# Three sets of projection buffers, a shorter weight path and a contention-aware order in a hybrid decoder layer

## The chip, the cores and the metric

The kernel runs on all 8 cores of one Trainium2 chip, one batch row on each core, with no exchange between cores. The time is device microseconds (us) of the slowest core of one execution. Cores 0 to 3 are one die, 4 to 7 the other. Some executions are of a slower state: part of the cores get a lower granted TensorE clock and are some per cent longer. Such executions are "slow".

Engines: PE is the matmul engine, PEld its weight load, DVE is VectorE, ACT is ScalarE, POOL is GpSimd, SP only issues transfers.

## The reference, cut to what matters

```python
# BATCH 8, SEQ 2048, D_MODEL 1024, 8 query / 2 key heads of 64, LRU_WIDTH 512, D_FF 2816
h = rmsnorm(x, norm_mix_pre)
q, k, v, lx, lg = split(h @ w_in)                     # 1792 columns
attn = sliding_window_attention(q, k, v, sinks)       # window 128, ALiBi, banded blocks of 128
lx = causal_dwconv(lx, lru_conv_w, lru_conv_b)        # 4 taps
lru = rg_lru(lx, wa, ba, wx, bx, lam) * gelu(lg)      # gates, exp, sqrt(1 - a^2), scan along SEQ
merged = concat(rmsnorm(attn, g_attn), rmsnorm(lru, g_lru))
x = x + rmsnorm(merged @ w_out, norm_mix_post)
f = rmsnorm(x, norm_ffn_pre) @ w_up                   # 5632 columns
gate, val = split(causal_dwconv(f, ffn_conv_w, b))    # 3 taps
x = x + rmsnorm((gelu(gate) * val) @ w_down, norm_ffn_post)
```

## The kernel before

The mixer (all up to the first residual) goes through four chunks of 512 positions. Each chunk has five stages: A (norm and transpose of x), B (projection with w_in), D (convolution, gates, scan), C (attention), E (output matmul, two norms, transposes for the FFN). The program builds a graph of operations with a priority (`key`) and, for each, the engines that could do it with a duration; a list scheduler in the same file places them and turns the graph into five in-order instruction streams. A dependency is a tile name, so one buffer under one name also orders the chunks that use it.

The w_in weights go through three f32 staging buffers and are multiplied by the norm gain on the way:

```python
    def stage(src, nbytes, key):
        i = ns[0] % 3
        ns[0] += 1
        dma("sp", stg[i][:], src, nbytes, [], ["stg%d" % i], key, ("stg", i))
        return stg[i], "stg%d" % i
    ...
    for n, fc in enumerate(order):
        s_, sk = stage(win_d[fc].rearrange("p c n -> p (c n)"), 524288, -50 + n)
        f = tt_fn(win[:, fc], s_[:].rearrange("p (c n) -> p c n", c=8), g0b, ALU.mult)
        P.op({"dve": (1.25, f), "pool": (2.4, f)}, [sk, "pp"], [("win", fc)], -50 + n)
```

There is one buffer of each projection result, and the chunks are written out one after the other:

```python
    hT = alloc("hT", [128, 8, 512], BF16)
    qT = alloc("qT", [128, 4, 512], BF16)
    glT = alloc("glT", [128, 4, 512], BF16)
    ...
    wout_load()
    for k in range(NCH):
        stage_a(k)
        stage_b(k)
        stage_d(k)
        stage_c(k)
        ...                                  # for k == 0: xe0, xe1, ye, h2b are placed
        stage_e(k)
```

The convolution reads its input from SBUF, and the output stage goes through one `ye` and one `h2b`:

```python
                for tap in (2, 1, 0):
                    sh = 3 - tap
                    stt(xc[:, cc, :], lx[:, c, o0 - sh:o0 - sh + 512], cw(c, tap), xc[:, cc, :], ALU.mult, ALU.add,
                        512, LXK + ["pp", (nm["xc"], cc)], [(nm["xc"], cc)], key)
    ...
            X, Y, H = xe[t % 2], ye, h2b     # stage_e
```

The softmax here doesn't subtract the row's maximum and nothing guards it: scores larger than these inputs give would overflow.

## Time and profile before

| | before |
|---|---|
| median of 17 executions, us, slow ones included (5 were there at first: 844.23) | 843.12 (839.92 to 919.5) |
| span of the profiled execution, slowest core, us | 840.2 |
| median span of the dies, us | 835.9 and 834.9 |
| PE / DVE / ACT / POOL busy, us | 708 / 487 / 391 / 335 |
| starts of the four output stages, us | 122.3, 205.9, 288.7, 393.0 |
| end of the last transpose for the FFN, us | 446.2 |
| up matmuls done before that end | 336 of 1408 |

The prediction below shows the lines for the main readings (busy tenths, windows, chain, waits). Two groups of the page matter besides. The columns are line, engine, operation, output and inputs, shapes, count, then busy us and mean ns of one, then the idle time just before them with what ended it:

```profile
L442 DVE SCALAR_TENSOR_TENSOR xc<-lx,pp,xc 128x512 f32<-128x512 bf16 x48 | 44.2, 939 | 2.4 <-POOL xc L432 1.2
L422 ACT ACT_TABLE_LOAD x27 | 34.6, 1283 | 20.3 <-DVE T L442 7.5
```

The first is the convolution taps, both tensor inputs in SBUF (the core's on-chip memory), 939 ns in the mean. The second is the activation table loads, 27 of them, with 20.3 us of idle time just ahead.

The last three rows of the table are my way to read a pipeline of stages. They come from the timeline of PE: the first matmul with `wob` of each chunk starts an output stage, and the last transpose with `h2b` ends the mixer. An "up matmul" is one of the 1408 with w_up, the first part of the FFN. After that, PE only has the rest of the FFN.

### The profile page before, as it was taken

The numbers are of one execution on the slowest core, as the hardware profiler recorded it, in microseconds if no ns is written. First come the engines' busy times: TensorE is split into PE (matmuls) and PEld (weight loads), VectorE is DVE, ScalarE is ACT, GpSimd is POOL, SyncE is SP. The second block draws the span as 40 slices with busy tenths as digits, with TensorE's granted clock in tenths as the row PEclk, the third lists the DMA queues.
The fourth block names the chain that finished last, engine by engine and source line by source line (L and its number), as shares of the span: only waits on it lengthen the run. The fifth ranks groups of instructions, "written<-read, shape, count | busy, mean of one in ns | idle before, by whom it ended". The sixth has DMA issues, their size and how long they took to land.

```text
span 840.2 us, 10795 instructions; the slowest of 8 cores (830.9 to 840.2 us)
## 1 busy us (share of the span) xinstructions
PE 708.3 (84%) x3700; PEld 330.7 (39%) x3700; DVE 487.0 (58%) x488; ACT 390.5 (46%) x534; POOL 334.7 (40%) x391
## 2 busy tenths in 40 slices
PE   0394878588848878589888999999999999999995
PEld 0141443334333433234333444444444444444442
DVE  2395854485448556856657777322377777772322
ACT  2247825882587359486344555111144444541111
POOL 4292372536253444736454444301044444442000
PEclk9997899698988999799989999999999999999998
DMA  9877112401320046787863444232254444411231
GB/s 216 257 230 217 52 51 106 144 1 51 114 86 1 2 125 176 106 133 103 186 174 66 79 79 78 53 122 103 101 126 76 75 76 76 76 26 50 101 113 62
DMA packets 25253, 85.52 MB, mean 102 GB/s; under 512 B 3056, under 2 KB 3440, under 8 KB 25072
## 3 DMA queue, kind: packets, MB, share of 16 engines
q0 software_dynamic: 10080, 29.66, 21.6%
q1 hardware_dynamic: 15120, 55.18, 20.0%
q8 instruction: 30, 0.49, 0.3%
q14 instruction: 23, 0.19, 0.1%
HBM read 97.70 MB, written 16.78 MB: 136 GB/s over the span
## 4 chain that ended last, share of the span: by engine, by line
PE 60%; DVE 9%; POOL 8%; issue 8%; ACT 7%; DMA 7%; SPq 0%; POOLq 0%; DVEq 0%; ACTq 0%
PE ps L461 59%; DMA stg<-w_in_r 4%; POOL stats L435 2%; DMA stg<-w_out_r 2%; DVE ye L442 2%; POOL stats L432 2%; POOL xe L435 1%; PE ps L466 1%; ACT xc L422 1%; DVE xc L706 1%; DVE xe L435 1%; ACT PT L422 1%; ACT h2b L422 1%; DVE T L442 1%; ACT L422 1%
## 5 line engine op out<-in xcount | busy, mean ns | idle before, releaser
L461 PE MATMUL ps<-h2T,wu 128*128 128x512 bf16 x1408 | 314.8, 385 | 17.8 <-DVE T L442 11.5
L442 DVE SCALAR_TENSOR_TENSOR T<-ps,pp,T 128x1023 f32<-128x1023 f32 (+1 forms) x176 | 223.9, 1280 | 68.9 <-ACT T L422 33.6
L461 PEld LDWEIGHTS ps<-h2T,wu 128*128 128x128 bf16 x1408 | 138.0, 99 | 188.8 <-issue 31.1
L422 ACT ACTIVATE T<-ps,pp 128x1024 f32<-128x1024 f32 x88 | 105.8, 1203 | 132.0 <-PE ps L461 130.0
L461 PE MATMUL ps<-wdn,uT 128*128 128x512 bf16 x704 | 152.3, 379 | 0.5 <-issue 0.5
L435 POOL TENSOR_TENSOR uT<-gg,T 128x1024 bf16<-128x1024 f32 x44 | 103.7, 2357 | 54.5 <-DVE T L442 49.0
L432 POOL TENSOR_SCALAR stats<-stats 128x1 f32<-128x1 f32 (+1 forms) x72 | 27.5, 381 | 209.5 <-ACT yf L422 128.4
L461 PE MATMUL ps<-hT,win 128*128 128x512 bf16 x416 | 100.5, 399 | 3.7 <-ACT hT L422 1.4
L461 PEld LDWEIGHTS ps<-wdn,uT 128*128 128x128 bf16 x704 | 68.8, 98 | 83.7 <-issue 0.9
L442 DVE SCALAR_TENSOR_TENSOR yf<-ps,stats,g 128x1024 f32<-128x1024 f32 x16 | 20.5, 1284 | 110.7 <-POOL stats L435 110.7
L422 ACT ACTIVATE yf<-ps 128x1024 f32<-128x1024 f32 x16 | 16.4, 1023 | 132.7 <-PE ps L461 132.7
L461 PEld LDWEIGHTS ps<-hT,win 128*128 128x128 bf16 x416 | 40.8, 101 | 54.9 <-issue 14.7
L422 ACT ACTIVATE gg<-T 128x1024 f32<-128x1024 f32 x44 | 46.3, 1053 | 12.7 <-DVE T L442 9.6
L435 POOL TENSOR_TENSOR stats<-stats,nhalf 128x1 f32<-128x1 f32 (+1 forms) x68 | 47.8, 703 | 9.1
L442 DVE SCALAR_TENSOR_TENSOR xc<-lx,pp,xc 128x512 f32<-128x512 bf16 x48 | 44.2, 939 | 2.4 <-POOL xc L432 1.2
L422 ACT ACT_TABLE_LOAD x27 | 34.6, 1283 | 20.3 <-DVE T L442 7.5
L466 PE MATMUL ps<-ident,hb 128*128 128x128 bf16 x128 | 14.8, 293 | 33.8 <-POOL hb L432 33.8
L442 DVE SCALAR_TENSOR_TENSOR h2b<-xe,stats,g 128x1024 bf16<-128x1024 f32 x16 | 22.6, 1411 | 35.2 <-POOL stats L435 35.2
L470 POOL DMA_DIRECT2D wu<-w_up_r x44 | 26.3, 597 | 40.9 <-PE ps L461 39.6
L442 DVE SCALAR_TENSOR_TENSOR ye<-ps,stats,g 128x1024 f32<-128x1024 f32 x16 | 20.5, 1284 | 30.6 <-POOL stats L435 30.6
L466 PE MATMUL ps<-ident,h2b 128*128 128x128 bf16 x128 | 12.0, 249 | 28.1 <-DVE h2b L442 12.1
L435 POOL TENSOR_TENSOR T<-T,carry 128x2 f32<-128x2 f32 x44 | 8.8, 200 | 66.4 <-DVE T L442 66.0
(103 smaller groups left out, 719.2 us busy)
## 6 DMA issues: line engine op xcount, KB each, us to landing
wu<-w_up_r POOLq DMA_DIRECT2D x44, 512.0 KB, 5.2
xt<-x SPq DMA_DIRECT2D x16, 512.0 KB, 5.0
xe<-x SPq DMA_DIRECT2D x16, 512.0 KB, 3.5
out<-xe SPq DMA_DIRECT2D x16, 512.0 KB, 2.7
xf<-out SPq DMA_DIRECT2D x16, 512.0 KB, 3.8
out<-xf SPq DMA_DIRECT2D x16, 512.0 KB, 2.7
stg<-w_in_r SPq DMA_DIRECT2D x14, 512.0 KB, 8.7
wdn<-w_down_r POOLq DMA_DIRECT2D x22, 256.0 KB, 8.9
```

Source lines behind the costliest of these rows:

```text
L422: return e.activation(**kw)
L432: return lambda e: e.tensor_scalar(out=_v(out), in0=_v(in0), scalar1=s1, scalar2=s2, op0=op0, op1=op1)
L435: return lambda e: e.tensor_tensor(out=_v(out), in0=_v(in0), in1=_v(in1), op=op)
L442: return P.op({"dve": (dur, lambda e: e.scalar_tensor_tensor(out=_v(out), in0=_v(in0), scalar=scalar, in1=_v(in1), op0=op0, op1=op1))}, re ...
L461: fns.append(lambda e, o=o, l=l, r=r, s0=s0, s1=s1: e.matmul(_v(o), lhsT=l, rhs=r, start=s0, stop=s1))
L466: fns = [lambda e, o=o, i=i: e.transpose(_v(o), i, ident[:]) for (o, i) in items]
L470: return P.op({eng: (0.6 if eng == "pool" else 0.08, lambda e: e.dma_start(out=out, in_=in_))}, reads, writes, key, dma=nbytes, slot=slot)
L706: P.op({"dve": (1.3, lambda e, cc=cc, init=init, a2=a2, tha=tha, thx=thx: e.tensor_tensor_scan(out=a2[:, cc, :], data0=tha[:, cc, :], data ...
```

## The change

Its intent is to fill PE in the mixer. It does these things together:

- w_in is cast by its transfers straight into place, the tables and later weights wait for pieces of it, and the gains move to the evictions of the transposes;
- three sets of `qT`, `xcb`, `glT` and two `hT`, with the projections of chunks 1, 2 and 3 written ahead of earlier chunks' later stages;
- the convolution runs on the projection's PSUM result, with a small carry for the three columns at a chunk's start;
- the square root becomes exp(0.5 ln), which leaves two activation table sets, and each load is issued ahead of the waits of its activation;
- the scheduler has better durations, a rule that keeps long DVE and POOL operations apart ("the lock rule"), and a penalty for the slower of two engines; two groups of transfers are moved in the order by hand.

The diff, cut to its core (`...` marks cuts; renamed keys, durations and the FFN's buffer places are left out):

```diff
+        def locked(o, e):
+            return e in lockt and len(o.alts[e]) > 2 and o.alts[e][2]
+        fastest = [min(a[0] for a in o.alts.values()) for o in ops]
 ...
+                    if locked(o, e):
+                        st = max(st, lockt["pool" if e == "dve" else "dve"])
 ...
-                if best is None or (pick[0], pick[1].key) < (best[0], best[2].key):
-                    best = (pick[0], e, pick[1])
+                pen = 0.7 * (pick[1].alts[e][0] - fastest[pick[1].idx])
+                if best is None or (pick[0] + pen, pick[1].key) < (best[3], best[2].key):
+                    best = (pick[0], e, pick[1], pick[0] + pen)
 ...
+                        if e == "act" and o.tload:
+                            eng.preload_act_table_set(TABSETS[o.tload])
 ...
+    for i in range(3):
+        INTO.append(cur[0])
+        qTs.append(alloc("qT%d" % i, [128, 4, 512], BF16))
+        xcbs.append(alloc("xcb%d" % i, [128, 4, 512], BF16))
+        glTs.append(alloc("glT%d" % i, [128, 4, 512], BF16))
+    hTs = [alloc("hT%d" % i, [128, 8, 512], BF16) for i in range(2)]
 ...
-    for n, fc in enumerate(order):
-        s_, sk = stage(win_d[fc].rearrange("p c n -> p (c n)"), 524288, -50 + n)
-        f = tt_fn(win[:, fc], s_[:].rearrange("p (c n) -> p c n", c=8), g0b, ALU.mult)
-        P.op({"dve": (1.25, f), "pool": (2.4, f)}, [sk, "pp"], [("win", fc)], -50 + n)
+    for n, fc in enumerate(order):
+        P.tag["win", n] = dma("pool", win[:, fc, :, :], win_d[fc], 524288, [], [("win", fc)], -50 + n, ("win", fc))
 ...
+                for tap in (2, 1):
+                    sh = 3 - tap
+                    stt(T[:, sh:512], pb(g, lambda a, sh=sh: a[:, 0:512 - sh]), cw(c, tap), T[:, sh:512],
+                        ALU.mult, ALU.add, 512, [g, tk, "pp"], [tk], key)
 ...
-            act(a2[:], a2[:], AF.Sqrt, 1024, XC, XC, key + 2, scale=-1.0, bias=1.0, tab=("sqrt",))
+            act(a2[:], a2[:], AF.Ln, 1024, A2, A2, key + 2, scale=-1.0, bias=1.0, tab=("L",))
+            act(a2[:], a2[:], AF.Exp, 1024, A2, A2, key + 2, scale=0.5, tab=("L",))
 ...
-    wout_load()
-    for k in range(NCH):
+    for k in range(3):
         stage_a(k)
         stage_b(k)
-        stage_d(k)
-        stage_c(k)
 ...
+    stage_d(0)
+    stage_c(0)
+    stage_a(3)
+    stage_b(3)
+    stage_e(0)
 ...
```

## The prediction

> **What bounds the kernel now.** I read the clock of the eight cores first (0.942 to 0.952 on both dies: an undisturbed run), then the page, then the windows. On the page, the busy tenths of the slowest core:
>
> ```profile
> PE   0394878588848878589888999999999999999995
> DVE  2395854485448556856657777322377777772322
> ACT  2247825882587359486344555111144444541111
> PEclk9997899698988999799989999999999999999998
> ```
>
> (One digit is 21 us.) PE is full in the right half, at full clock. In the left half no engine is full for long, and the granted clock dips with the holes. The windows view, cut where the character changes, gives the budget:
>
> ```profile
> 0.00:94.00 94.00, 45.55 (x277) 22.11 (x278) 51.66 (x72) 42.69 (x65) 41.62 (x46) 0.91 0.78 217
> 94.00:446.00 352.00, 277.82 (x1653) 134.65 (x1649) 217.95 (x246) 211.20 (x312) 170.69 (x199) 0.90 0.40 95
> 446.00:831.70 385.70, 384.90 (x1778) 173.89 (x1776) 214.88 (x170) 135.51 (x156) 121.65 (x144) 1.00 0.36 81
> 831.70:840.20 8.50, 0.00 (x0) 0.00 (x0) 2.51 (x2) 1.11 (x2) 0.74 (x2) 0.65 0.15 62
> ```
>
> Columns: stretch, length, then busy us of PE, weight load, DVE, ACT, POOL, then clock, DMA share, GB/s. Start (94 us): the DMA is busy 78%. Mixer (352 us): PE 79%, DVE 62%, ACT 60%, clock 0.90; nobody is the bound, they wait for each other. FFN (386 us): PE 99.8%; only fewer matmuls would shorten it. Tail 8.5 us.
>
> The chain that ended last says what the start waits for: weights staged in f32 through three buffers, scaled on DVE or POOL, and the next staging load held back by that scaling.
>
> ```profile
> 3.76 16.02 DMA stg<-w_in_r
> ...
> 21.89 10.95 DMA stg<-w_in_r
> ...
> 59.55 5.43 DMA stg<-w_out_r
> ...
> 73.12 6.52 DMA stg<-w_out_r
> ```
>
> In the mixer stretch the waits view is a ring of short handoffs, and table loads (22 of 27 are there) stand on the chain:
>
> ```profile
> POOL stats L432 <- ACT h2b L422: 40.1, 12, 4.5
> DVE h2b L442 <- POOL stats L435: 35.2, 13, 6.2
> DVE ye L442 <- POOL stats L435: 30.6, 16, 5.6
> ```
>
> Projection buffers (hT, qT, glT) are single, so the next chunk's projection, which would fill PE, cannot run while this chunk's recurrence, attention and output stage pass around that ring. In the chain, the output stage of chunks 0 to 3 starts at 122, 206, 289 and 393 us: a period of 83 us and more.
>
> **What the Trainium skill says.** "ScalarE: Activation LUTs", section "What ACT_TABLE_LOAD costs": about 1283 ns, whatever the set. The trace agrees: 27 loads at a mean of 1283 ns. Its section "Table sets" has exp and ln together in one set, which is what lets the change write the square root as exp(0.5 ln). "TensorE: Matmul & The Clock Gate", section "Back-to-back issue gap": N/2.4 + 2.5 ns, 216 ns at N = 512, in isolation, and less in a sustained stream (131 ns). The trace sides with the first: 187 recorded in a full 40 us window is 214 ns each. "VectorE: DVE Perf Modes", section "Two Vector instructions with no wait between them", has the second SBUF read interface shared with GpSimd, used by ops with two SBUF tensors. The trace fits that: the convolution taps with both tensors in SBUF took 939 ns for 512 columns, while the FFN taps with one tensor in PSUM took 1280 ns for 1023, so some 0.75 us for 512. "DMA: Bandwidth & Descriptors", section "SWDGE vs HWDGE vs iDMA": a cast in flight needs GpSimd's queue. The wu loads already do it, 5.2 us to landing.
>
> **The change, part by part.**
>
> (1) Start. w_in is cast by the DMA straight into its place; the gain moves to the eviction of the transpose. Off go 9 x 1.56 + 5 x 2.06 = 24 us of DVE and POOL work and the three-buffer ring. The bytes stay: 14 x 0.5 MB plus four x tiles of 0.5 MB, 9.4 MB. At the 217 to 257 GB/s of the first slices that is about 40 us, so w_in is complete at about 44 us instead of 58, and the first projection ends near 48. Then comes a catch: on the SP queue the x tiles 6 and 7 stand behind three w_out loads and gbc, and those wait for the last w_in piece. These 3.7 MB take 15 us more; with norm and transposes the second projection starts at about 66 us, where the kernel before got to it at 94. Gain 28 us.
>
> (2) PE work for the rest. Matmul counts do not change. At 0.2157 us: projection 416 = 90, gates 32 = 7, scores 124 = 27, output 256 = 55; V, PV, transposes about 43. Mixer sum 222 us at full clock; FFN 2112 x 0.2157 = 456. The order on PE has 208 up matmuls (45 us) ahead of the last transpose of the last output stage, where before it was some 330 (71 us, from 456 less the 385 of the FFN stretch). So the mixer stretch has 222 + 45 less the 33 done before 66 us = 234 us of full-clock PE work, against some 257 before (check: 277.8 busy x clock 0.90 = 250).
>
> (3) DVE in the mixer, order counts times durations of the rows before. Convolution: 63 us (48 x 0.94, 9 + 9 helpers, 8 lx evictions) becomes 48 x 0.75 = 36. Gain-carrying evictions: 15 become 32 x 1.23 = 39. h2b 22.6 becomes 11 x 0.8 = 9; hb 0 becomes 7; the attention normalisation, now in halves, costs 8 more; w_in off 14. The sum is about 224 against 222: no relief in total. After 66 us some 201 are left, plus 33 for FFN taps: 234, as much as PE.
>
> (4) ACT. 27 loads become 20: minus 9. Convolution start plus 12.6, ln and exp for sqrt plus 8.4, norm scalings plus 7; lx and transposed evictions minus 19. No net change, some 211 us. But each load is now issued ahead of the waits of its activation, so a part of them is hidden. POOL loses some 35 us.
>
> (5) Where the gain really comes from: three sets of qT, xcb, glT and two of hT. On PE's order, projections of chunks 2 and 3 now lie between the score, gate and output matmuls of the chunk before. The stretch becomes limited by throughput (234 us for PE at full clock, 234 for DVE) rather than by the ring. It still has E stages with one ye and one h2b buffer, and for chunks 1 and 2 four output groups back to back on PE which leave at the pace of that one buffer, so PE will not be full. I take 90% PE busy (79% before) and clock 0.92 (0.90): 234 / 0.83 = 282 us.
>
> (6) FFN: 1904 matmuls remain after the last transpose: 411 us. gelu now writes in place, which holds a T buffer until POOL's 2.36 us product is done. A buffer is held some 10 us and two steps take 2 x 16 x 2 x 0.2157 = 13.8, so this hides. Tail 8.5.
>
> Sum: 66 + 282 + 411 + 8.5 = 767. I put 765.
>
> **The rivals.**
> (a) The ring persists: E stages and the recurrence set the period whatever PE has to fill in, or DVE's in-order queue, with conv, gains and FFN taps mixed, holds short links of the chain behind long ones. For it: DVE's sum did not fall, and the gain evictions are now on DVE alone (before, 10 of 32 went to ACT). Then density stays at 0.79 x 0.90: 234 / 0.71 = 329, and the time is 815.
> (b) The order is nearly perfect: better-measured durations (a four-column power is now booked at 1.4 us; the trace has 1.28 and 1.5, the old order assumed 0.35), DVE and POOL kept off each other. 95% busy at clock 0.95 gives 259, and 744.
> (c) The start does not get shorter: transfers of all cores share the memory, and POOL's queue now issues both w_in and the statistics. Then 20 us are lost: 785. Against it: the start is one stretch where bytes alone need 40 us and the kernel took 58.
> (d) The clock: denser matmuls could meet a lower granted clock on all cores. The FFN stretch at 99.8% busy had 1.00, which speaks against it.
>
> **Range and chances.** (a) in part and (c) in part make the upper end, 800; (b) the lower, 735. For no gain of 2% (827) the mixer would have to become looser than before while also starting later; chances 0.96 faster, 0.03 same, 0.01 slower.
>
> **What would show it.** Right: PE continuously busy from about 66 us; the last transpose of h2b at about 345 to 350 us, with DVE near 83% and PE near 90% between; convolution taps near 0.75 us; 20 table loads; the last 420 us as full as before. Wrong: second projection after 80 us (step 1); output stages of successive chunks still 80 us apart or PE under 80% in the mixer (step 5); holes in the FFN stretch (step 6); granted clock under 0.95 there (d).

## The result, and the profile after

The changed kernel is correct and takes 770.66 us (median of 9 executions, 769.84 to 775.89; one more, of 779.24, is not among the nine). A ratio here is the mean time of one kernel's fast runs over that of the other's in the same rounds, so it is not quite the ratio of the medians quoted. It is 0.917 (95% interval 0.915 to 0.919). The profiled execution has a span of 768.8 us, all cores between 761.8 and 768.8 us at a clock of 0.963 to 0.974: an undisturbed run, like that of before.

The busy tenths of the changed kernel's slowest core (one digit is now 19 us):

```profile
PE   1887987898899699989999999999999999999995
...
DVE  3536677854686769687777762223777777752222
ACT  3267889765788766555555441111545455431111
...
PEclk9996999899799879999999999999999999999998
```

PE is at 7 to 9 tenths from the second slice on, with one dip to 6. The windows view, cut at the second projection and at the last transpose, has the same columns as in the prediction:

```profile
0.00:66.60 66.60, 39.56 (x228) 19.98 (x228) 31.26 (x60) 33.98 (x55) 22.98 (x51) 0.93 0.96 222
66.60:347.70 281.10, 252.82 (x1569) 117.88 (x1570) 199.78 (x291) 203.58 (x305) 131.08 (x196) 0.93 0.45 111
347.70:759.40 411.70, 411.15 (x1905) 186.05 (x1902) 234.77 (x184) 150.19 (x176) 133.32 (x153) 1.00 0.38 85
759.40:768.80 9.40, 0.00 (x0) 0.00 (x0) 2.51 (x2) 1.11 (x2) 0.74 (x2) 0.73 0.14 57
```

From 66.6 us to the last transpose PE is busy 252.8 / 281.1 = 90% at clock 0.93. The FFN stretch is as full as before and longer, because more of its matmuls are left.

The start in the chain of the changed kernel:

```profile
2.89 13.74 DMA xe<-x
...
23.08 17.40 PE ps L491 x72
...
41.05 1.15 ACT hb L452 x2
...
44.20 12.02 DMA xt<-x
...
66.65 21.89 PE ps L491 x128
```

The first projection starts at 23 us (before: 36). The second starts at 66.65 us, where the kernel before got to it at 93.98. Between them stands a 12 us load of two x tiles. It starts late because its buffer is freed by tiles 4 and 5, whose squares (`hb`, at 41.05) stood in ACT's in-order queue behind evictions of the first projection.

The waits of the mixer, where the prediction showed 40.1, 35.2 and 30.6 us:

```profile
POOL stats L462 <- ACT h2b L452: 41.3, 12, 4.5
DVE h2b L462 <- POOL stats L465: 19.3, 10, 3.4
...
DVE ye L472 <- POOL stats L465: 11.1, 11, 2.5
```

The waits for the statistics got shorter, the wait of the statistics for ACT did not. PE stands still less for any of them: its largest single entry in the view of PE's own waits is 3.8 us in this stretch, where before it was 12.1 us.

And the two groups shown of before:

```profile
L472 DVE SCALAR_TENSOR_TENSOR ct<-ps,pp,ct 128x510 f32<-128x510 f32 x16 | 11.9, 746 | 0.9
L389 ACT ACT_TABLE_LOAD x20 | 25.7, 1283 | 1.4 <-PEq L418 1.1
```

A tap takes 746 ns in place of 939 in the mean; there are 20 loads in place of 27, and idle time just ahead of them is nearly gone.

The mean of 939 ns hides two kinds of taps, which the prediction took for one. In the trace of before, 33 of the 48 taps take 720 to 754 ns, as short as those from PSUM (the matmul's result memory) now. The other 15 take 0.91 to 2.37 us; each of them lies beside a POOL operation on wide SBUF tensors (512 columns or more) and ends 0.54 or 0.55 us after it. One such pair, from the timelines of DVE and of POOL:

```profile
55.97 2.37 DVE L442 SCALAR_TENSOR_TENSOR xc<-lx,pp,xc 128x512 f32<-128x512 bf16 x1
```

```profile
55.74 2.06 POOL L435 TENSOR_TENSOR win<-stg,pp 128x1024 bf16<-128x1024 f32 x1
```

So reading from PSUM did not make the tap itself faster; it took the tap out of POOL's way. In a run below without the lock rule, 11 of these taps start while such a POOL operation runs, and they still take 733 to 746 ns.

Where did the 71 us between the two profiled spans come from? The last transpose ends at 347.8 us in place of 446.2: 98.4 us earlier. But 128 fewer up matmuls had been done by then (208 against 336), and at the 0.2157 us each of the full stretch those are paid back later: 27.6 us. The difference, 70.8 us, is the gain (71.4 us) to within 1 us. So the question is what brought the last transpose forward. The output stages of the four chunks:

| kernel | output stages start at, us | last transpose ends, us | up matmuls before it |
|---|---|---|---|
| before | 122.3, 205.9, 288.7, 393.0 | 446.2 | 336 |
| changed | 109.0, 173.2, 240.0, 307.6 | 347.8 | 208 |

The first stage is only 13.3 us earlier. The rest is the period: 83 to 104 us before, 64 to 68 us now.

### The profile page after: what moved, and what is told of

Read it like the earlier page. It is cut to its first block, busy times and chain, and to the rows that moved or that the text cites. A ratio compares the mean times of both kernels' runs of the same rounds, so it can differ in the third digit from the quotient of the medians.

```text
span 768.8 us, 10924 instructions; the slowest of 8 cores (761.8 to 768.8 us)
## 1 busy us (share of the span) xinstructions
PE 703.5 (92%) x3700; PEld 323.9 (42%) x3700; DVE 468.3 (61%) x537; ACT 388.9 (51%) x538; POOL 288.1 (37%) x400
## 4 chain that ended last, share of the span: by engine, by line
PE 82%; issue 4%; DVE 4%; ACT 4%; DMA 3%; POOL 2%; SPq 0%; POOLq 0%; DVEq 0%; ACTq 0%
PE ps L491 80%; PE ps L496 2%; DMA xe<-x 2%; DMA xt<-x 2%; DVE ye L472 1%; POOL stats L465 1%; POOL stats L462 1%; ACT h2b L452 1%; DVE hT L465 1%; ACT hb L452 0%; DVE T L472 0%; DVE h2T L465 0%; ACT PT L452 0%; ACT a L452 0%; DVE xe L465 0%
## 5 line engine op out<-in xcount | busy, mean ns | idle before, releaser
L491 PE MATMUL ps<-h2T,wu 128*128 128x512 bf16 x1408 | 305.5, 379 | 2.9 <-DVE h2T L465 1.7
L465 POOL TENSOR_TENSOR uT<-T 128x1024 bf16<-128x1024 f32 x44 | 103.7, 2357 | 68.6 <-DVE T L472 62.7
L462 POOL TENSOR_SCALAR stats<-stats 128x1 f32<-128x1 f32 (+1 forms) x72 | 21.2, 295 | 224.1 <-ACT yf L452 128.4
L472 DVE SCALAR_TENSOR_TENSOR yf<-ps,stats,gbc 128x1024 f32<-128x1024 f32 x16 | 20.5, 1284 | 110.7 <-POOL stats L465 110.7
L491 PEld LDWEIGHTS ps<-hT,win 128*128 128x128 bf16 x416 | 40.5, 102 | 58.1 <-issue 19.8
L452 ACT ACTIVATE T<-T 128x1024 f32<-128x1024 f32 x44 | 46.2, 1051 | 3.9 <-POOL T L465 3.2
L452 ACT ACTIVATE PT<-ps 128x1024 bf16<-128x1024 f32 (+1 forms) x32 | 31.3, 989 | 16.3 <-PE ps L491 16.2
L491 PE MATMUL ps<-wob,lruT 128*128 128x512 bf16 x128 | 30.2, 379 | 0.1
L491 PE MATMUL ps<-wob,attnT 128*128 128x512 bf16 x128 | 30.2, 379 | 0.0
L491 PE MATMUL ps<-etab,ident 128*128 128x512 bf16 x62 | 22.4, 446 | 6.5 <-DVE dsm L854 1.5
L452 ACT ACTIVATE h2b<-xe 128x1024 bf16<-128x1024 f32 x16 | 16.8, 1053 | 22.6 <-DVE xe L465 18.4
```

The costliest lines, as they stand in the source:

```text
L452: return e.activation(**kw)
L462: return lambda e: e.tensor_scalar(out=_v(out), in0=_v(in0), scalar1=s1, scalar2=s2, op0=op0, op1=op1)
L465: return lambda e: e.tensor_tensor(out=_v(out), in0=_v(in0), in1=_v(in1), op=op)
L472: return P.op({"dve": (dur, lambda e: e.scalar_tensor_tensor(out=_v(out), in0=_v(in0), scalar=scalar, in1=_v(in1), op0=op0, op1=op1), lock ...
L491: fns.append(lambda e, o=o, l=l, r=r, s0=s0, s1=s1: e.matmul(_v(o), lhsT=l, rhs=r, start=s0, stop=s1))
```

## The experiments

My theory was that of the prediction: the extra buffers let the next projections fill the ring's holes, the earlier start adds 28 us, and hidden table loads a little. The rivals: the scheduler's new order makes the gain, not the buffers; and an earlier start is not passed on. Each run below was correct. The first four shared one chip and one set of runs of the kernel before (median 840.51 us), then four (855.75 us, mostly slow; its three fast runs 839.93 to 841.17), then three (840.60), then the last (840.95).

### One set of buffers

```diff
-        par, b = k % 2, k % 3
+        par, b = 0, 0
 ...                                   # stages of each chunk in turn again, one hT
-         VCAP = 4
+         VCAP = 3                     # the list scheduler could not place it with 4
```

(The changed kernel's own instruction order is identical with either value of `VCAP`, so this is no second change.)

> The changed kernel with a single set of qT, xcb, glT and a single hT, chunks written down one after another as in the kernel before; start, table sets, convolution, gains and scheduling rules stay. Theory (buffers): the mixer falls back to the ring of handoffs; of the 72 us gained, 28 are the start and the other 44 come back: 805 to 820 us, first 512-column projection of chunk 1 late again, PE under 85% busy between chunk 1's projection and the last transpose. Rival (order): the better durations and the DVE/POOL rule made the mixer denser, the buffers little: under 785 us.

It took 813.2 us (median; fast runs 812.43 and 801.03, the latter with all cores at 0.944 or more), ratio 0.961 (0.949 to 0.972), in which the 812.43 has one pair of cores at a clock of 0.925. Core 3 of its profile is undisturbed (clock 0.951). There, the stretch that answers to the changed kernel's 252.8 us of PE work and clock 0.93 is:

```profile
66.60:347.70 281.10, 236.72 (x1435) 108.12 (x1434) 179.69 (x267) 179.72 (x276) 114.34 (x174) 0.89 0.38 93
```

PE does 1435 matmuls here in place of 1569, busy for 84% of the time in place of 90%, at a clock of 0.89. Output stages start at 97.7, 197.4, 255.2 and 337.2 us. I had expected the second projection to be late again; it was not, and starts at 64.0 us. The buffers are worth about 32 us: six undisturbed cores of this run have 796.8 to 800.6 us, the dies of the changed kernel 766. So my theory held for the buffers, but it leaves a little more, from 835 to 799, to the rest.

### Two sets

```diff
-        par, b = k % 2, k % 3
+        par, b = k % 2, k % 2
 ...                                   # B of chunk 2 written after C of chunk 0, B of chunk 3 after C of chunk 1
```

> The changed kernel with two sets of qT, xcb, glT (projection one chunk ahead instead of two). Theory (buffers): one chunk ahead is nearly all of it: 768 to 780 us. Rival (order): no different from the changed kernel or from the one-set kernel, all three within 5 us.

Its fast runs took 769.68 and 769.96 us (four of six were slow, at 787 to 789), ratio 0.917 (0.914 to 0.919): that of the changed kernel. Its output stages start at 107.8, 172.4, 239.3 and 307.0 us. The third set is worth nothing measurable.

### Table loads behind the waits

```diff
-                        if e == "act" and o.tload:
-                            eng.preload_act_table_set(TABSETS[o.tload])
                         for p in o.waits:
 ...
+                        if e == "act" and o.tload:
+                            eng.preload_act_table_set(TABSETS[o.tload])
```

> The changed kernel with each table load issued behind the waits of its activation instead of ahead of them; the order of all other instructions is the same. Theory (hidden loads count): of 20 loads of 1.28 us only those whose activation waits for something can hide, and only some of them lie on the path: 2 to 8 us slower. Rival (ACT is off the path or always late): within 1 us.

Of five runs one was fast, at 768.97 us; four were slow (785.8 to 787.4), so there is no interval. The loads do wait again:

```profile
L395 ACT ACT_TABLE_LOAD x20 | 25.7, 1283 | 8.1 <-DVE dp L465 4.4
```

Idle time ahead of them is 8.1 us in place of 1.4, and the one fast time is below the changed kernel's lowest, 769.84. My theory fell: hiding the loads buys nothing that this run shows. There was little to hide: of the 8.1 us, 4.4 stand ahead of the first load, at the start, and 3.4 ahead of three others; the remaining 16 follow the activation before them without a wait.

### Own buffers for x tiles 6 and 7

This takes away the late 12 us load of the start.

```diff
+    xq = [P.tile("xq%d" % i, [128, D], F32, L0 + 4096 * i) for i in range(2)]
 ...
+            if k == 1 and tl >= 2:
+                X, xk = xq[tl - 2], "xq%d" % (tl - 2)
```

> The changed kernel with buffers of their own for x tiles 6 and 7, loaded once the tenth w_in piece is in, so no longer behind the w_out loads and the norm of tiles 4 and 5. Theory (the catch of the start, prediction step 1): chunk 1's projection starts at 52 to 57 us instead of 66.6, and 8 to 12 us of it reach the end: 758 to 763 us. Rival (the mixer is bound by chunk 0's own recurrence and attention, or the bytes just arrive elsewhere): within 3 us of the changed kernel.

Fast runs took 771.46 to 772.42 us, ratio 0.919 (0.917 to 0.921): no gain. From PE's timeline of this run, the lines of the second projection and of the first output stage:

```profile
57.05 1.89 PE L491 MATMUL ps<-hT,win 128*128 128x512 bf16 x8 [1.62 <-DVE hT L465]
...
124.35 1.89 PE L491 MATMUL ps<-wob,lruT 128*128 128x512 bf16 x8
```

The second projection came 9.6 us earlier, but the first output stage 15 us later (124.35 against 109.0), and the last transpose ends at 348.9 against 347.8. The start can be moved without moving the end. The rival held.

### The new scheduler on the old graph

```diff
 # the kernel before, with: locked(), pen, the new durations, lock flags on long DVE and POOL operations,
 # and table loads booked ahead of their activations (in the plan alone)
-        P.op({"pool": (0.35, tt_fn(rs, s1, nhalf[:, 0:n], ALU.pow))}, ...
+        P.op({"pool": (0.35 + 0.26 * n, tt_fn(rs, s1, nhalf[:, 0:n], ALU.pow))}, ...
```

> The kernel before with nothing but the list scheduler of the changed kernel: its new durations, its rule that keeps long operations of VectorE and GpSimd apart, and its priorities; buffers, start and w_in path are those of before, and no activation table is loaded ahead. If the order that the scheduler finds is itself worth much, this falls under 800 us. If, as the one-set run says, a longer distance between tiles needs the buffers, it lands at 820 to 845 us with stages of about 90 us between the starts of successive output matmuls.

It took 833.47 us (832.28 to 857.24), but in all four runs a pair or more of cores were at a low clock, so no ratio is given. Its profile: cores 0, 1, 4 and 5 at a clock of 0.948 to 0.954 took 806.6 to 814.4 us, the others at 0.919 to 0.926 took 824.6 to 830.1. Core against core at full clock, the order alone is worth about 25 us (835 to 810). On core 4, output stages start at 114.1, 187.7, 268.2 and 367.5 us, 84 us apart in the mean (before: 90). The time lies where the buffer theory put it, but with disturbed cores; the undisturbed ones lie between my two ranges. I had given the order nothing, and it has about a third of the whole gain. The lock rule works here too: on core 4 only three of the 48 taps take more than 0.8 us, where before it was 15.

### The new start on the old graph

```diff
-        s_, sk = stage(win_d[fc].rearrange("p c n -> p (c n)"), 524288, -50 + n)
-        f = tt_fn(win[:, fc], s_[:].rearrange("p (c n) -> p c n", c=8), g0b, ALU.mult)
+        dma("pool", win[:, fc, :, :], win_d[fc], 524288, [], [("win", fc)], -50 + n, ("win", fc))
 ...
+            P.op({"dve": (1.23, tt_fn(hT[:, :, tl * 128:(tl + 1) * 128], ..., g0b, ALU.mult))},   # gain at the eviction
 ...                                   # the first three w_out loads and gbc wait for the last w_in piece
```

> The kernel before with only the start of the changed one: w_in is cast by its transfer and put in place, the gain is applied on the eviction of hT, and the later weights wait for the last piece of w_in. My prediction's first step says that the whole gain at the start (about 28 us) reaches the end: 812 to 822 us. The rival, from the run with own x buffers, where a start 9.6 us earlier moved the end by nothing, is that an earlier start is not passed on because the period of the stages sets the end: 830 to 845 us.

All six runs were slow, 847.88 to 853.61 us, so neither range can be checked by the time. In the profile two cores, 6 and 7, were undisturbed (clock 0.94 and 0.948): 825.8 and 825.2 us, some 10 us less than the 835 of before. On core 6 the second projection starts at 86.5 us and on core 7 at 87.2; in the kernel before it was 92.7 us on core 1 and 94.0 on core 7. That is 5.5 to 7.5 us and not 28. So the weight path alone does not bring the second projection forward by much: the x tiles, their norms and the order have to follow. These few us were not passed on either: on core 7 the first output stage starts at 122.4 us (before: 121.2 us on core 1, 122.3 on core 7) and the last transpose ends at 442.1 us (before: 438.8 and 446.2). What these cores gained are 48 more up matmuls done by then, 384 against 336, which are 10.4 us. So this run agrees with the one with own x buffers: an earlier second projection alone does not move the output stages. Why more up matmuls fitted in I did not test.

### The changed kernel without the lock rule and the penalty, and with one of them

```diff
             def locked(o, e):
-                return e in lockt and len(o.alts[e]) > 2 and o.alts[e][2]
+                return False                                          # rule off
 ...
-                pen = 0.7 * (pick[1].alts[e][0] - fastest[pick[1].idx])
+                pen = 0.0                                              # penalty off
```

Both off:

> The changed kernel, its scheduler without the rule that keeps long VectorE and GpSimd operations apart and without the lengthened durations that it reckons with. If that rule is worth what the shorter VectorE rows suggest (conv taps 939 to 745 ns, scans 1563 to 1269 ns), this run has taps near 900 ns again and is 10 to 30 us slower: 780 to 800 us. If VectorE does not set the period of the stages, it is within 6 us of the changed kernel's 770 us.

Rule kept, penalty off:

> The changed kernel whose scheduler keeps the rule that long VectorE and GpSimd operations don't overlap, but places an operation on whichever engine is free first, without the penalty for the slower one. The run without both took 788 us. If the penalty was the part that mattered (long work sent to GpSimd at 2.4 us in place of 1.2 us), this stays at 780 to 790; if the rule was, it is at 768 to 775.

Penalty kept, rule off:

> The counterpart: penalty kept, rule dropped. If the rule was what mattered, this is at 780 to 790 us with scans near 1380 ns as in the run without both; if the penalty was, it is at 768 to 775 us.

| kernel | median, us | ratio to before (95%) | output stages start at, us | scans, ns |
|---|---|---|---|---|
| both (the changed kernel) | 770.66 | 0.917 (0.915 to 0.919) | 109.0, 173.2, 240.0, 307.6 | 1269 |
| rule alone | 778.98 | 0.926 (0.924 to 0.928) | 97.1, 190.4, 244.3, 305.4 | 1398 |
| penalty alone | 783.56 | 0.933 (0.931 to 0.934) | 105.1, 179.6, 240.2, 319.3 | 1598 |
| neither | 788.28 | 0.938 (0.935 to 0.941) | 107.3, 197.1, 253.1, 306.8 | 1383 |

(Scans are the twelve with a carried state, mean of one. The text of the run with neither speaks of lengthened durations; its edit takes away the rule and the penalty, and the durations stay.) So the two are worth some 18 us together, and neither makes up the whole. My expectations were half right. The run with neither is as slow as I said, but its taps took 741 ns, not 900: in the changed kernel taps read PSUM and do not need the rule (the 11 that start beside a wide POOL operation here take 733 to 746 ns). In the single runs I had one of the two matter; both do.

That the rule is about two engines getting in each other's way can be seen in single instructions. From the timelines of POOL and of DVE in the run with the penalty alone:

```profile
194.91 2.35 POOL L465 TENSOR_TENSOR xe<-xe,ye 128x1024 f32<-128x1024 f32 x1 [1.59 <-DVE ye L472]
```

```profile
195.82 2.52 DVE L783 TENSOR_TENSOR_SCAN a<-tha,hst,thx 128x512 f32<-128x512 f32 x1
198.26 0.15 DVE L854 RECIPROCAL dsm<-dsm 128x4 f32<-128x4 f32 x1
198.33 1.25 DVE L783 TENSOR_TENSOR_SCAN a<-tha,hst,thx 128x512 f32<-128x512 f32 x1
```

The first scan falls beside a POOL sum of two SBUF tensors and takes 2.52 us; its twin right after takes 1.25. POOL's operation ends at 194.91 + 2.35 = 197.26, and the scan ends 1.08 us later, which is nearly a scan's whole duration: it looks as if it had stood until POOL was done. The Trainium skill, "SBUF — State Buffer", section "SBUF: two separate sides", says so: the pair of ports that both engines share is "an exclusive lock, not a bandwidth split", and the later one waits. This pair of lines agrees, and so do the others: of the 16 scans of that run, five take more than 1.3 us, and each of them starts while a wide POOL operation runs and ends 1.06 to 1.08 us after it. Two scans that started before such an operation kept their 1.26 and 1.27 us. In the changed kernel no scan lies beside one, and all 16 take 1.19 to 1.28 us. With the rule alone, the mean of 1398 ns comes from a single scan of 2.84 us beside a sum on POOL: the rule works on planned times, and the chip's differ. Against the changed kernel, this run's longer scans and gate products are some 9 us of DVE time (12 x 0.33, 7 x 0.53 and 8 x 0.14 us, an estimate from the means), out of 13 us between the two. The order that comes out is another one as well, with output stages at other times. How much each of these two weighs I did not separate.

### A second ye and h2b in the place of the third set

```diff
-            X, Y, H = xe[t % 2], ye, h2b
+            X, Y, H = [xe[0], xe[1], xe2][t % NXE], [ye, ye1][t % 2], [h2b, h2b1][t % 2]
 ...                                   # two sets, and own x buffers for tiles 6 and 7 as above;
 ...                                   # B of chunk 2 is written ahead of E of chunk 0
```

> Two sets in place of three, and the space of the third given to own x buffers for tiles 6 and 7, a second buffer for ye and h2b, and a third for xe; same priorities. If the one ye and h2b buffer paces the stages after the output matmul, the period falls from about 67 us and the run is at 755 to 768 us. If the mixer is held by the busy time of PE and the clock, it is within 3 us of 770.

It took 764.78 us (764.3 to 765.78), ratio 0.910 (0.908 to 0.912), 6 us less than the changed kernel: its last transpose ends 2.5 us earlier with 16 more up matmuls done (3.5 us). The own x buffers and the two sets had each given nothing alone, so I put the 6 us down to the output stage's buffers (`ye`, `h2b` and a third `xe`); they were not tried apart. POOL's wait for `h2b` fell from 41.3 to 18.4 us. The stretch from 66.6 us to the last transpose (345.2 us) has PE 251.48 / 278.6 = 90% busy, as before.

### The same with other priorities, and these priorities alone

```diff
-    KA = [-60, 5, 105, 205]           # norm and transposes of chunks 0 to 3
-    KB = [10, 110, 210, 310]          # projection
-    KD = [20, 120, 220, 320]          # recurrence
-    KC = [22, 122, 222, 322]          # attention
-    KE = [60, 160, 260, 360]          # output stage
+    KA = [-60, 5, 109, 205]
+    KB = [10, 110, 206, 314]
+    KD = [38, 120, 220, 320]
+    KC = [20, 122, 157, 322]
+    KE = [85, 160, 216, 312]
```

With the buffers of the run above:

> The run with more h2 buffers (764.8 us), with the priorities of attention, recurrence and output stages of tiles 1 to 3 moved so that the next projection and output stage come earlier. If the remaining time in the mixer is a matter of order, this is 745 to 758 us; if PE's work and the granted clock hold it, it stays within 5 us of 764.8.

On the changed kernel's buffers:

> The changed kernel, three sets and its one ye and h2b buffer kept, with only the priorities of the retuned run. If the 20.6 us between the run with more h2 buffers and the retuned one are a matter of order alone, they come here too: 745 to 755 us. If the earlier output stages need the second ye and h2b buffer, little comes: 763 to 775 us.

With the buffers: 744.18 us (743.67 to 744.8), ratio 0.886 (0.884 to 0.887), faster than both kernels and just under my range. Without them: 778.09 us, ratio 0.926 (0.924 to 0.928), slower than the changed kernel, which neither of my ranges had. The windows of the fast one, to its last transpose at 322.2 us and to the end of the matmuls:

```profile
66.60:322.20 255.60, 239.79 (x1534) 114.87 (x1534) 203.70 (x291) 197.21 (x299) 126.83 (x191) 0.95 0.49 123
322.20:735.00 412.80, 411.11 (x1904) 186.05 (x1902) 234.78 (x185) 150.87 (x178) 133.23 (x152) 1.00 0.37 84
```

PE is 94% busy at clock 0.95 (changed kernel: 90% and 0.93), and the last transpose comes 25.6 us earlier with the same 208 up matmuls done. That is the 25.5 us between the two profiled spans (768.8 and 743.3). With one `ye` and `h2b`, the same priorities start the last output stage early too (295.5 us), but it then takes 64 us to the last transpose (359.7), against 37 us (285.1 to 322.2) with two. So the gain of this order came only with the other buffers (two sets, own x buffers and a third `xe` among them). That the single `ye` and `h2b` make those 64 us, with two output stages close together, fits but was not tested by itself. The waits for it, with two buffers and without:

```profile
POOL stats L462 <- ACT h2b L452: 13.6, 8, 4.2
...
DVE ye L472 <- POOL stats L465: 5.2, 9, 0.9
```

```profile
POOL stats L462 <- ACT h2b L452: 37.1, 13, 6.2
...
DVE ye L472 <- POOL stats L465: 18.2, 12, 5.6
```

## Why the prediction was right, and where it was not

The predicted time was 765, and 770.66 was measured; the range held it. By its own steps:

1. Start. The second projection at "about 66 us" came at 66.65, but the reason was in part another. The chain names the buffer of tiles 4 and 5, held by ACT's queue until 44.1 us; the w_out loads and gbc, issued from 40.5 us, came before x tiles 6 and 7 on the queue and moved at the same time. That this is a gain of 28 us in a sum was wrong. The first output stage came only 13.3 us earlier, moving the second projection by another 9.6 us moved the end by nothing, and the weight path alone moved it by 5.5 to 7.5 us and the first output stage not at all. The sum came out since the stretch after 66 us was reckoned from the same point.
2. PE work of the mixer, 234 us at full clock: 252.82 x 0.93 = 235.
3. DVE. Mixer work was to be 224 us; it is 202 (31.26 + 199.78 less the 29.0 of 23 FFN taps), 83% predicted in the stretch, 71% measured. Most of that was a wrong sum: the parts that the prediction lists (63 to 36, 15 to 39, 22.6 to 9, 0 to 7, plus 8, minus 14) take 222 us to 206, not to 224. The tap was right (0.75 us), as was the gain eviction (1.22). But the reading of the tap was not: 0.75 us is what a tap with both tensors in SBUF takes as well when POOL is not beside it. What I left out are the other operations with two SBUF inputs, which got shorter as fewer stood beside POOL: carried scans 1563 to 1269 ns, gate products 1389 to about 1228, some 6 us together.
4. ACT. 20 loads as said. That "a part of them is hidden" is true of four of them at most, and worth nothing in the run that tried it. ACT is the fullest engine after PE in places: 69.6 of 80 us between 60 and 140 us. Whether it paces that stretch I did not test.
5. Mixer stretch. 90% and 0.92 were a choice; 90% and 0.93 were measured, and 281.1 us for 282. That this choice fitted so well is luck in part: DVE's load was off by a seventh, the order's share was not in it, and the sum shows none of this. And the cause was incomplete. Two sets do what I gave to three. And of the 70 us or so between undisturbed cores (835 to 766), the one-set run leaves 32 to the buffers. The other 37 were there without them: about 25 with the scheduler alone, about 10 with the start alone (as 48 up matmuls done earlier, not as an earlier output stage). That these nearly add up is no proof; the convolution from PSUM and the two table sets, which the one-set kernel has too, were not tried apart. The prediction had the order only as rival (b), an extra.
6. FFN. 1904 matmuls and 411 us predicted, 1905 and 411.7 measured; gelu in place hides. The tail was 9.4, not 8.5.

The rivals: (a), one ring at the old density, is near what the one-set run made of it (801 to 813, predicted 815). (b), the nearly perfect order, was 744; the changed kernel is not that, but the retuned one with more buffers is, at 744.18 and with 94% and 0.95 for the predicted 95% and 0.95. (c) did not happen; (d) did not: the clock of the full stretch stayed at 1.00.

## What to carry to other kernels

Where stages pass work around a ring, read the gain from the period between the same stage of successive chunks and from what of the later phase no longer overlaps, not from the sum of starts. Buffers and priorities can be worth little apart and much together: the same priorities gave 20 us with the second output buffers and what came with them, and lost 7 without. Before adding a third buffer try two, and give the freed space to the stage that still has one. And look at single durations before reading a mean: here a mean of 939 ns was 33 short taps and 15 that waited.

## What the Trainium skill lacked or had wrong

- "TensorE: Matmul & The Clock Gate", section "Back-to-back issue gap", has 131 ns for a matmul of 512 columns in a sustained stream. In the full FFN stretch of the changed kernel 1905 matmuls took 411.15 us: 216 ns each.
- The same page, section "Seeing it yourself", has the clock of a whole die fall to 13/16 once three of its cores run dense matmuls. Here all eight cores ran 385 us of matmuls, PE recorded busy for 373.85 us of them or more, at a clock of 0.99 to 1.00 in the profile before. A die near that clock shows in some slow executions only (cores 0 to 3 at 0.802 to 0.828 in the one-set run of 911.75 us, the other die at 0.944 to 0.947). Where a low clock showed, it came in pairs of neighbouring cores (0.919 to 0.926 on cores 2, 3, 6 and 7 of the scheduler run's profile, beside 0.948 to 0.954 on the others), so that half a die could have it; no page has this.
- "ScalarE: Activation LUTs", section "What ACT_TABLE_LOAD costs", has 1283 ns and 1380 ns more of drain for a switch. The 1283 ns are in the trace; the drain is not. In the changed kernel a load starts at 43.25 us, 0.02 us after the instruction before it ends, lasts 1.28, and the next activation starts at 44.54.
- No page has what running a load ahead of its activation's waits is worth. Here idle time ahead of the loads fell from 8.1 to 1.4 us and the time did not fall (768.97 us in the one fast run with the loads behind, 770.66 with them ahead).
